# First norm's gain spread by TensorE into PSUM, the first v products issued singly, and a new order for the first stage

## The chip, the cores and the metric

The kernel runs on one core of one Trainium2 chip. A core has TensorE (PE; its weight loads are shown as PEld), VectorE (DVE), ScalarE (ACT), GpSimd (POOL) and SyncE (SP), which here only issues transfers; 16 DMA engines move data between HBM and SBUF. TensorE writes to PSUM, eight banks of 128 x 512 fp32 words. The metric is the device time of one execution in microseconds. Lower is better.

## The reference, cut to what matters

One layer of a decoder trunk over 1024 tokens of width 1024, all in float32:

```python
h = rms_norm(x, norm1_g)                       # x * rsqrt(mean(x*x) + eps) * g
q, k, v, glu_a, glu_b = split(h @ w_in)        # 512 columns each
attn = stick_breaking_attention(norm(q), norm(k), v)       # 8 heads x 64, causal
c = silu(layer_norm(causal_depthwise_conv(glu_a * sigmoid(glu_b))))   # width 31
x = x + concat([attn, c]) @ w_out
h = rms_norm(x, norm2_g)
gate, val = split(h @ w_up)                    # 2816 columns each
x = x + (silu(causal_dwconv3(gate)) * val) @ w_down
```

## The kernel before

Tokens lie in eight tiles of 128 (`t`), the model width in eight tiles of 128 (`k`). Every float32 product is made of three float32r matmuls (`mm3`, lines 387 to 390): each operand is split into a high part (`hi`, a cast on ACT) and a low part (`lo`, the source less the high part, on DVE or POOL), and hi x hi, hi x lo and lo x hi are added up in PSUM. So a product cannot run before the parts that it reads are made.

The first stage, up to about 420 us, holds the first norm, the five input projections, the convolution, the attention and the convolution's half of the output projection. After it come the second norm with the rest of the output projection, then the up projection (`u`, `u_S`) and the down projection (`dn`), each by a recursive block scheme.

At the start the gain of the first norm, one row of 4 KB in HBM, is read once for each of the 128 partitions (line 445), which is a transfer of 512 KB on ACT's queue into `g1`. PE meanwhile runs 16 idle matmuls on zeros (line 477). SP issues the loads of the eight tiles of x (`load_x`, line 485, 512 KB each) and of the weights (`weights`, line 538, 512 KB for each of the four v weights). A token tile then goes through `norm_in` (line 488): ACT squares it with a running sum (L494), into the tiles `attn` and `attn_first` in turn, which are scratch at that time; POOL makes the reciprocal root (`rstd`, L379 and L380); DVE scales the whole tile by the root and by `g1` (L498, 1024 elements in a partition); PE transposes it in two groups of four (L507); ACT copies each group out as the high part (L511), and DVE subtracts for the low part (L512). `weights` casts the high part on ACT (L542) and makes the low part on DVE or POOL (L547).

`project` (line 653) multiplies a token tile with the weights. For each of the eight `k` it adds one operation of three matmuls, which waits for the weight's low part (`ready`) and for the low part of that half of h. The v result goes out of PSUM in one copy of two pieces (L592).

The order of the work in the first two stages is written out. Each operation is given to a planner (`Plan`, line 146) with an engine or a choice of engines, a cost, what it waits for and the buffers it takes (`Token`). The planner's `run` goes through a table of operation numbers (`ORDERS`, line 61), which count in the order of `add`, picks an engine and a buffer by its costs, and emits. Within PE, DVE, ACT and POOL the emitted order is then fixed (`in_order`). The costs decide only engine and buffer; waits on the chip come from the data.

The banks named `z` (two) carry the convolution's two running sums (`conv_a`, L762) and later the attention's scores; `s` (three) carry transposes, `o` (three) the projections.

Of the kernel before, what the change touches and what calls it, by code (L numbers as in the profile page):

```python
# [8 lines left out]
F32 = mybir.dt.float32  # L9
# [24 lines left out]
CONV_AT = 52  # L34
V_AT = (12, 17.5, 45, 50.5, 78, 83.5, 89, 94.5)
# [235 lines left out]
def kernel(  # L271
# [192 lines left out]
    def in_order(start_at):  # L464
        last = {}
        for ins in nc.cur_bb.bb.instructions[start_at:]:
            if ins.engine in ORDERED:
# [3 lines left out]
                last[ins.engine] = ins  # L471

    start_at = len(nc.cur_bb.bb.instructions)
    idle = ps_.tile([P, 4, P], F32, tag="s2", name="idle")

    for i in range(16):
        nc.tensor.matmul(idle, ident_b, zero_b.unsqueeze(1).to_broadcast([P, 4, P]), start=True, stop=True)
# [1479 lines left out]
```

## Time and profile before

| | us |
|---|---|
| median of 3 runs | 1114.17 (1113.96 to 1115.74) |
| the profiled execution | 1114.16 |
| its span | 1112.4 |
| TensorE busy | 1092.3, 98% of the span |
| VectorE busy | 885.6, 80% |
| ScalarE busy | 608.7, 55% |
| GpSimd busy | 565.6, 51% |

The profile shows one execution. A line such as L498 is a line of the kernel before. Busy PE counts idle matmuls too, and it counts a matmul longer while PE's clock is granted at half rate. Matmuls are pipelined: their durations overlap, so the distance from start to start is what one costs. A stretch's row gives the length, then each engine's busy time and number of instructions, the granted PE clock, the share of time in which the DMA engines were busy, and GB/s. A piece of the chain of waits is a start, a length and the work that ended last.

### The profile page before, as it was taken

Reading aid. Unit: us, or ns where it says so; the run is one execution under the profiler, and the core shown is the slowest. Engines: PE = TensorE matmul, PEld = TensorE weight load, DVE = VectorE, ACT = ScalarE, POOL = GpSimd, SP = SyncE. Lnnn points to the kernel's source line nnn. Section 1 sums busy time; section 2 is a strip of 40 time slices with the busy share of each in tenths; the row PEclk is TensorE's granted clock in tenths of the full one; section 3 lists DMA queues with packets and bytes.
Section 4 is the critical chain, followed back from the end, with each engine's and each line's share of the span. In section 5 each row is a group of like instructions: output and inputs, shape, how many; then the busy total and the mean of one; then the engine's idle time right before and its main releaser. Section 6 shows DMA issues by size and latency. Waiting matters only on the chain.

```text
span 1112.4 us, 14919 instructions
## 1 busy us (share of the span) xinstructions
PE 1092.3 (98%) x5255; PEld 907.1 (82%) x5255; DVE 885.6 (80%) x1181; ACT 608.7 (55%) x1139; POOL 565.6 (51%) x509
## 2 busy tenths in 40 slices
PE   7999999999999999989999999999999999999998
PEld 5887888778888887768888888888888888888887
DVE  5587999679997996988886777677777578797795
ACT  6354467897766674654343434333333388776660
POOL 3064579677455452765333133223322199888770
PEclk9999999999999999999999999999999999999999
DMA  8111410353824216532322222223132482403404
GB/s 295 38 32 29 123 39 5 91 173 87 268 72 150 86 44 203 170 95 77 114 84 87 77 95 76 95 65 106 58 99 72 152 321 77 151 20 133 151 4 149
DMA packets 110233, 118.52 MB, mean 107 GB/s; under 512 B 21105, under 2 KB 89936, under 8 KB 110158
## 3 DMA queue, kind: packets, MB, share of 16 engines
q1 hardware_dynamic: 110014, 117.05, 32.1%
q8 instruction: 41, 0.67, 0.3%
q10 hardware_dynamic: 144, 0.52, 0.1%
q14 instruction: 34, 0.28, 0.1%
HBM read 82.95 MB, written 28.31 MB: 100 GB/s over the span
## 4 chain that ended last, share of the span: by engine, by line
PE 86%; POOL 5%; DVE 3%; ACT 2%; issue 2%; DMA 1%; SPq 0%; POOLq 0%; DVEq 0%; ACTq 0%
PE dn L1916 19%; PE u_S L388 7%; PE u_S L390 7%; PE u_S L389 7%; PE u L390 5%; PE u L389 5%; PE u L388 5%; PE po L1315 3%; POOL attn L789 3%; PE wT L1287 3%; PE z L1238 2%; PE z L1239 1%; PE op L388 1%; PE op L389 1%; PE op L390 1%
## 5 line engine op out<-in xcount | busy, mean ns | idle before, releaser
L1916 PE MATMUL dn<-wd,wd 128*128 128x512 f32 x768 | 181.4, 389 | 0.0
L1916 PEld LDWEIGHTS dn<-wd,wd 128*128 128x128 f32 x768 | 144.1, 188 | 29.9
L1919 DVE TENSOR_TENSOR c<-dn,c 128x512 f32<-128x512 f32 x120 | 81.7, 687 | 27.4 <-PE dn L1916 26.7
L389 PE MATMUL u_S<-bT,aS 128*128 128x512 f32 x264 | 102.7, 389 | 0.0
L390 PE MATMUL u_S<-bT,aS 128*128 128x512 f32 x264 | 102.7, 389 | 0.0
L388 PE MATMUL u_S<-bT,aS 128*128 128x512 f32 x264 | 102.4, 389 | 0.0
L384 ACT CAST aS<-rawu 128x512 fp32r<-128x512 f32 x63 | 38.9, 621 | 95.0 <-PE u_S L390 67.6
L1821 ACT CAST wd<-rawd 128x512 fp32r<-128x512 f32 x128 | 72.7, 618 | 31.8 <-DMA rawd<-act_d 8.4
L1260 DVE TENSOR_TENSOR_SCAN nb<-nb,one 128x896 f32<-128x896 f32 (+7 forms) x64 | 85.1, 1342 | 1.6 <-ACT nb L1246 1.3
L1662 POOL TENSOR_TENSOR s<-rawu 128x512 f32<-128x512 f32 x21 | 29.5, 1406 | 95.0 <-DMA rawu<-in_w_up_dram 93.8
L1820 ACT COPY whole<-rawd 128x512 f32<-128x512 f32 x110 | 63.4, 585 | 24.6 <-DVE wd L1822 11.9
L1668 POOL TENSOR_TENSOR rawu<-rawu 128x512 f32<-128x512 f32 x21 | 28.4, 1354 | 86.7 <-DVE a L385 86.7
L1822 DVE TENSOR_TENSOR wd<-whole,wd 128x512 fp32r<-128x512 f32 x90 | 60.1, 686 | 12.5 <-ACT wd L1821 6.2
L789 POOL TENSOR_TENSOR attn<-attn,attn_first 128x512 f32<-128x512 f32 x42 | 48.5, 1156 | 40.8 <-ACT attn L779 32.4
L390 PE MATMUL u<-b,a 128*128 128x512 f32 x168 | 65.5, 390 | 1.5 <-DVE a L385 1.5
L1265 POOL TENSOR_SCALAR nb<-nb 128x896 f32<-128x896 f32 (+7 forms) x52 | 37.6, 724 | 57.3 <-DVE nb L1260 44.7
L1765 DVE SCALAR_TENSOR_TENSOR y<-gv,cols_a,y 128x1023 f32<-128x1023 f32 (+1 forms) x44 | 59.2, 1345 | 8.5 <-ACT y L1763 8.4
L388 PE MATMUL u<-b,a 128*128 128x512 f32 x168 | 65.5, 390 | 0.0
L389 PE MATMUL u<-b,a 128*128 128x512 f32 x168 | 65.4, 389 | 0.0
L384 ACT CAST a<-rawu 128x512 fp32r<-128x512 f32 x63 | 39.0, 620 | 45.6 <-PE u_S L390 31.8
L390 PEld LDWEIGHTS u_S<-bT,aS 128*128 128x128 f32 x264 | 49.6, 188 | 10.3
L389 PEld LDWEIGHTS u_S<-bT,aS 128*128 128x128 f32 x264 | 49.5, 188 | 10.3
(339 smaller groups left out, 3239.0 us busy)
## 6 DMA issues: line engine op xcount, KB each, us to landing
rawu<-in_w_up_dram SPq DMA_DIRECT2D x44, 512.0 KB
act_d<-y SPq DMA_DIRECT2D x22, 512.0 KB
rawd<-act_d SPq DMA_DIRECT2D x22, 512.0 KB
rawd<-in_w_down_dram SPq DMA_DIRECT2D x22, 512.0 KB
raw_qk<-in_w_in_dram SPq DMA_DIRECT2D x16, 256.0 KB
rawo<-in_w_out_dram SPq DMA_DIRECT2D x8, 512.0 KB
m<-conv_d SPq DMA_DIRECT2D x16, 256.0 KB
xt<-in_x_dram SPq DMA_DIRECT2D x8, 512.0 KB
```

The lines of the kernel that those rows point to most:

```text
L384: nc.scalar.copy(hi, src)
L388: nc.tensor.matmul(ps, a_hi, b_hi, start=first, stop=False)
L389: nc.tensor.matmul(ps, a_hi, b_lo, start=False, stop=False)
L390: nc.tensor.matmul(ps, a_lo, b_hi, start=False, stop=last)
L789: last = add("POOL", 1092, lambda e=e: nc.gpsimd.tensor_tensor(d["c"], d["c"], e["t"], op=ALU.add), key(m, 16), [x, last])
L1260: nc.vector.tensor_tensor_scan(rev, rev, ones_of[0][:, :w], 0.0, op0=ALU.mult, op1=ALU.max)
L1765: nc.vector.scalar_tensor_tensor(y[:, j:], g[:, :S - j], par("fw", (KF - 1 - j) * NF + f), y[:, j:], op0=ALU.mult, op1=ALU.add)
L1820: nc.scalar.copy(whole, src)
L1821: nc.scalar.copy(t[:, 0], src)
L1822: lo_engine.tensor_tensor(t[:, 1], whole, f32(t[:, 0]), op=ALU.subtract)
L1916: nc.tensor.matmul(ps, a[:, tok], b, start=first and m == 0, stop=last and m == 2, skip_group_check=True)
L1919: nc.vector.tensor_tensor(sums[c][s], ps, sums[c][s], op=ALU.add)
```

## The change

- The gain is loaded as one row into partition 0 (`gain`), and a row of 128 ones (`gain_one`) is set by DVE. Two fp32 matmuls of one partition multiply the ones with each half of the row, so that each of the two `z` banks holds half of the gain on all partitions. PE runs five idle matmuls ahead of them and two behind, as the plan's first operation (`begin`), in place of the 16.
- `norm_in` scales a token tile in two halves of 512 elements, on DVE, with the gain read from PSUM; each half has its own transposes behind it.
- For token tiles 0 and 1 the v products are 24 single matmuls each, which wait only for the parts that they read (`high` or `ready` of the weight, `h_high` or `h_ready` of h). After the first, their order is free, and the copy out waits for all of them.
- The table of the first stage is new: 1915 numbers for 1874. Through the operations that are added, most numbers shift; the order changes in the whole stage. The table of the second stage stays.
- Some of the planner's costs change: the first transfer's start (4200 to 2900), a weight piece's issue, latency and transfer, and the costs of the two operations that take the attention result out of PSUM.

```diff
+SINGLE = (0, 1)
...
-    ROWS, PIECE, COLUMNS, MIXED, TWICE, FEW = (360, 1500, 1300), (430, 2000, 770), (390, 2050, 1650), (460, 2200, 870), (630, 1950, 450), (450, 1900, 50)
+    ROWS, PIECE, COLUMNS, MIXED, TWICE, FEW = (360, 1500, 1300), (430, 2200, 800), (390, 2050, 1650), (460, 2200, 870), (630, 1950, 450), (450, 1900, 50)
...
-    g1, sums_b = attn_row(0), attn_row(3)[:, S - P:]
-    nc.scalar.dma_start(g1, norm1_g.to_broadcast([P, D]))
+    sums_b = attn_row(3)[:, S - P:]
+    gain, gain_one = attn_row(3)[0:1, :], attn_row(2)[0:1, :P]
+    nc.scalar.dma_start(gain, norm1_g)
+    nc.vector.memset(gain_one, 1.0)
...
-                 in_turn=("nb", "wt", "th", "tl", "thd", "tld", "kst", "vst", "q", "qd"), dma=4200.0)
+                 in_turn=("nb", "wt", "th", "tl", "thd", "tld", "kst", "vst", "q", "qd"), dma=2900.0)
...
-    idle = ps_.tile([P, 4, P], F32, tag="s2", name="idle")
-    for i in range(16):
-        nc.tensor.matmul(idle, ident_b, zero_b.unsqueeze(1).to_broadcast([P, 4, P]), start=True, stop=True)
+    g1 = []
+    def begin():
+        idle = ps_.tile([P, 4, P], F32, tag="s2", name="idle")
+        def wait(n):
+            for _ in range(n):
+                nc.tensor.matmul(idle, ident_b, zero_b.unsqueeze(1).to_broadcast([P, 4, P]), start=True, stop=True)
+        wait(5)
+        for i, z in enumerate(gain_banks):
+            g1.append(bank(z, [P, HS], f"gain{i}"))
+            nc.tensor.matmul(g1[i], gain_one, gain[:, i * HS:(i + 1) * HS], start=True, stop=True)
+        wait(2)
...
+    gain_banks = [plan.token("z") for _ in range(2)]
+    gain_ready = add("PE", 6300, begin, -100.0, [], gain_banks)
...
-        c = add("DVE2", 1290, lambda: nc.vector.scalar_tensor_tensor(xt, xt, d["rs"], g1, op0=ALU.mult, op1=ALU.mult), T(at_), [b])
...
         for i in range(2):
+            cols = slice(i * HS, (i + 1) * HS)
+            c = add("DVE", 690, lambda i=i, cols=cols: nc.vector.scalar_tensor_tensor(xt[:, cols], xt[:, cols], d["rs"], g1[i], op0=ALU.mult, op1=ALU.mult),
+                    T(at_), [b, gain_ready])
+            gain_banks[i].users += [c]
...
+        singles = []
+        for k, which in ((k, which) for k in range(ND) for which in ("hh", "hl", "lh") if name == "v" and t in SINGLE):
+            def product(k=k, which=which):
...
+                nc.tensor.matmul(d["ps"], (h_hi if which[0] == "h" else h_lo)[t // 4][:, k, tok],
+                                 ws[k // 2]["hi" if which[1] == "h" else "lo"].rearrange("p k b c -> p k (b c)")[:, k % 2, :],
+                                 start=d["n"] == 1, stop=d["n"] == 3 * ND)
+            needs = [ws[k // 2]["high" if which[1] == "h" else "ready"], (h_high if which[0] == "h" else h_ready)[t][k // 4]]
+            singles.append(add("PE", 227, product, T(at_ + 0.7 * k), needs + singles[:1], [] if singles else [o]))
...
-                a = add("ACT", 580, copied, i + 0.3, [last, prev_last] + conv_normed + (on_diagonal[0] if blk else []))
-                b = add("DVE", 690, summed, i + 0.3, [a])
+                a = add("ACT", 690, copied, i + 0.3, [last, prev_last] + conv_normed + (on_diagonal[0] if blk else []))
+                b = add("DVE", 790, summed, i + 0.3, [a])
```

More of the change, by code (lines that the diff above doesn't have):

```diff
@@ L473 @@
     start_at = len(nc.cur_bb.bb.instructions)
-    idle = ps_.tile([P, 4, P], F32, tag="s2", name="idle")
-    for i in range(16):
-        nc.tensor.matmul(idle, ident_b, zero_b.unsqueeze(1).to_broadcast([P, 4, P]), start=True, stop=True)
+    g1 = []
[9 more added lines that the diff above has]
+        wait(2)
     done, big, nbs, ones_of, qkv = {}, {}, [None] * 4, [], {}
-    h_ready = {}
+    gain_banks = [plan.token("z") for _ in range(2)]
+    gain_ready = add("PE", 6300, begin, -100.0, [], gain_banks)
+    h_ready, h_high = {}, {}
     def load_x(t, key):
@@ L497, in norm_in @@
         b = add("POOL", 850, lambda: rstd(d["rs"], d["sq"], 1.0 / D), T(at_), [a])
-        c = add("DVE2", 1290, lambda: nc.vector.scalar_tensor_tensor(xt, xt, d["rs"], g1, op0=ALU.mult, op1=ALU.mult), T(at_), [b])
-        r.users += [c]
-        h_ready[t] = []
+        h_ready[t], h_high[t] = [], []
         for i in range(2):
+            cols = slice(i * HS, (i + 1) * HS)
+            c = add("DVE", 690, lambda i=i, cols=cols: nc.vector.scalar_tensor_tensor(xt[:, cols], xt[:, cols], d["rs"], g1[i], op0=ALU.mult, op1=ALU.mult),
+                    T(at_), [b, gain_ready])
+            gain_banks[i].users += [c]
+            r.users += [c]
             s = plan.token("s")
@@ L509, in norm_in @@
             where = (slice(None), slice(4 * i, 4 * i + 4), slice((t % 4) * P, (t % 4 + 1) * P))
-            a = add("PE", 440, turn, T(at_ + 1), [c], [s])
-            b = add("ACT", 600, lambda i=i, where=where: nc.scalar.copy(h_hi[t // 4][where], d["pt", i]), T(at_ + 1), [a])
+            m = add("PE", 440, turn, T(at_ + 1), [c], [s])
+            f = add("ACT", 600, lambda i=i, where=where: nc.scalar.copy(h_hi[t // 4][where], d["pt", i]), T(at_ + 1), [m])
             e = add("DVE", 690, lambda i=i, where=where: nc.vector.tensor_tensor(
-                h_lo[t // 4][where], d["pt", i], f32(h_hi[t // 4][where]), op=ALU.subtract), T(at_ + 1), [b])
-            s.users += [b, e]
+                h_lo[t // 4][where], d["pt", i], f32(h_hi[t // 4][where]), op=ALU.subtract), T(at_ + 1), [f])
+            s.users += [f, e]
             h_ready[t].append(e)
-        norm_done.append(a)
+            h_high[t].append(f)
+        norm_done.append(m)
     norm_done = []
@@ L549, in weights @@
         room.users += [x, a, b]
-        d["ready"] = b
+        d["high"], d["ready"] = a, b
         return d
@@ L653, in project @@
     def project(name, parts, ws, t, at_, room):
-        o, d, m = plan.token("o"), {}, None
+        o, d, m = plan.token("o"), {"n": 0}, None
         tok = slice((t % 4) * P, (t % 4 + 1) * P)
-        for k in range(ND):
+        singles = []
+        for k, which in ((k, which) for k in range(ND) for which in ("hh", "hl", "lh") if name == "v" and t in SINGLE):
+            def product(k=k, which=which):
+                if d["n"] == 0:
+                    d["ps"] = bank(o, [P, 512], f"{name}{t}")
+                    room()
+                d["n"] += 1
+                nc.tensor.matmul(d["ps"], (h_hi if which[0] == "h" else h_lo)[t // 4][:, k, tok],
[3 more added lines that the diff above has]
+            singles.append(add("PE", 227, product, T(at_ + 0.7 * k), needs + singles[:1], [] if singles else [o]))
+            for r in ws[k // 2]["rooms"]:
+                r.users += singles[-1:]
+        for k in range(ND if not singles else 0):
             def products(k=k):
@@ L675, in project @@
             return (summed if t in SUMMED_FIRST else normalized)(f"{name}{t}", d, o, m, to, at_ + 6)
-        a = add({"ACT": 700, "DVE": 800}, lambda eng: copy_out(eng, to(), d["ps"]), T(at_ + 6), [m])
+        a = add({"ACT": 700, "DVE": 800}, lambda eng: copy_out(eng, to(), d["ps"]), T(at_ + 6), singles or [m])
         o.users += [a]
```

146 rows, old and new, of the table ORDERS are left out of this document.

## The prediction

> **What bounds the kernel now.** I read the page's busy table first, then the table of stretches, then the chain of waits in the first 22 us, then the timeline there. The page and the stretches (columns: stretch, its length, busy time of PE, PEld, DVE, ACT, POOL with counts, granted clock, DMA share, GB/s):
>
> ```profile
> PE 1092.3 (98%) x5255; PEld 907.1 (82%) x5255; DVE 885.6 (80%) x1181; ACT 608.7 (55%) x1139; POOL 565.6 (51%) x509
> ```
>
> ```profile
> 0.00:10.00 10.00, 5.11 (x16) 1.87 (x16) 1.77 (x6) 4.29 (x7) 2.51 (x10) 1.00 0.79 272
> ...
> 30.00:100.00 70.00, 69.80 (x323) 57.28 (x322) 48.72 (x69) 25.77 (x45) 21.05 (x19) 1.00 0.11 31
> 100.00:120.00 20.00, 19.31 (x86) 15.66 (x85) 19.54 (x24) 13.02 (x20) 17.76 (x15) 1.00 0.36 99
> ...
> 200.00:300.00 100.00, 97.18 (x578) 82.31 (x578) 84.69 (x116) 83.29 (x205) 64.64 (x78) 1.00 0.50 156
> 300.00:400.00 100.00, 99.95 (x662) 88.80 (x662) 89.17 (x109) 69.15 (x143) 50.65 (x58) 1.00 0.32 96
> 400.00:500.00 100.00, 94.06 (x473) 77.22 (x472) 84.51 (x113) 56.72 (x108) 53.60 (x56) 0.98 0.45 142
> ```
>
> ```profile
> 10.14:21.52 11.38, 9.75 (x45) 7.34 (x45) 10.71 (x10) 8.55 (x14) 6.59 (x6) 0.85 1.05 384
> ...
> 22.00:70.00 48.00, 48.00 (x231) 39.57 (x230) 30.89 (x44) 22.51 (x38) 11.80 (x17) 1.00 0.17 48
> ```
>
> TensorE is the bound, with some 20 us of gaps in the span of 1112.4 us. Half of these lie ahead of 21.52 us, and those gaps are understated: the 5.11 us of the first row are idle matmuls, and the second table's clock of 0.85 over 11.38 us means 3.4 us at half rate. From 21.52 us PE runs without a gap to 70 us. So the first question is when PE becomes unbroken, and how much useful work it has done by then. The chain of waits of the first 23 us (start, length, what):
>
> ```profile
> 1.54 6.35 issue
> ...
> 8.21 0.57 POOL rs L380
> 8.78 0.03 issue
> 8.80 1.29 DVE x_k L498
> 10.10 0.04 issue
> 10.14 0.67 PE hT L507 x4
> ...
> 17.45 1.81 DVE x_q L498
> ...
> 20.79 0.69 DVE h_lo L512
> ```
>
> The first token tile's square (below) starts at 6.70, when x0 lands; its norm feeds the first transposes at 10.14. The last stall ends at 21.52, behind a scaling of x that held DVE from 17.45 on. In the timeline (start, length, engine, line, what, [idle before and releaser]):
>
> ```profile
> 6.70 1.06 ACT L494 ACTIVATE attn<-x_k 128x1024 f32<-128x1024 f32 x1 [4.05 <-DMA x_k<-in_x_dram]
> 7.94 1.06 ACT L494 ACTIVATE attn_first<-x_k 128x1024 f32<-128x1024 f32 x1
> 9.50 1.05 ACT L542 CAST hi_v<-raw_v 128x1024 fp32r<-128x1024 f32 x1 [0.41 <-DMA raw_v<-in_w_in_dram]
> 10.58 1.23 DVE L547 TENSOR_TENSOR lo_v<-raw_v,hi_v 128x1024 fp32r<-128x1024 f32 x1 [0.49 <-ACT hi_v L542]
> 10.83 0.59 ACT L511 CAST h_hi<-hT 128x512 fp32r<-128x512 f32 x1 [0.29 <-PE hT L507]
> 11.47 0.76 PE L388 MATMUL v<-hi_v,h_hi 128*128 128x512 f32 x1 [0.24 <-ACT h_hi L511]
> 11.72 0.68 DVE L512 TENSOR_TENSOR h_lo<-hT,h_hi 128x512 fp32r<-128x512 f32 x1
> 17.38 2.40 POOL L547 TENSOR_TENSOR lo_v<-raw_v,hi_v 128x1024 fp32r<-128x1024 f32 x1
> 17.45 3.42 DVE L498 SCALAR_TENSOR_TENSOR x_q<-x_q,rs,attn 128x1024 f32<-128x1024 f32 x1
> ```
>
> ```profile
> 22.71 0.60 PE L507 MATMUL hT<-ident_r,x_q 128*128 128x128 f32 x4
> 23.07 0.48 PE L388 MATMUL v<-hi_v,h_hi 128*128 128x512 f32 x1
> ...
> 24.08 0.39 PE L389 MATMUL v<-lo_v,h_hi 128*128 128x512 f32 x1
> 24.31 0.39 PE L390 MATMUL v<-hi_v,h_lo 128*128 128x512 f32 x1
> ```
>
> By start to start, a product costs 0.23 us and a group of four transposes 0.36. The 45 PE instructions between 10.14 and 21.52 are 24 transposes and 21 products: 6 x 0.36 + 21 x 0.23 = 7.0 us of work. So at 21.52 PE has lost 21.52 - 7.0 = **14.5 us**. The forecast is this loss after the change.
>
> **The change, part by part.** *The gain's load.* The spread row (queue q10) goes through the same 16 engines as x0. Bytes by queue in 2 to 6 us, then the total of 6 to 14 us:
>
> ```profile
> q1 hardware_dynamic: 175, 0.66, 48.6%
> q10 hardware_dynamic: 138, 0.51, 34.5%
> ```
>
> ```profile
> DMA packets 2028, 3.07 MB, mean 383 GB/s; under 512 B 146, under 2 KB 1657, under 8 KB 2028
> ```
>
> Without its 0.51 MB all loads behind come 0.51 / 383 = 1.33 us earlier at the most; at the least 0, if x0 is held by start-up and not by rate. DMA was full from 4 us on, so I take 1.25.
>
> *The gain's matmuls.* Sixteen idle matmuls become five, two gain products, two more idle ones: by the diff fewer idle matmuls, whatever the summary says.
>
> ```profile
> 1.68 5.11 PE L477 MATMUL idle<-zero_b,ident_b 128*128 128x512 bf16 x16 [1.68 <-DVE ident_b L341]
> ...
> 3.36 0.15 PEld L477 LDWEIGHTS <-ident_b 128*128 128x128 bf16 x1 [0.28 <-issue]
> 3.79 0.15 PEld L477 LDWEIGHTS <-ident_b 128*128 128x128 bf16 x1 [0.28 <-issue]
> ```
>
> At first they come 0.43 apart, so five end at 3.8. No row has a one-partition f32 product. Bounds: 0.23 each (a warm product) and 1.7 (four times the slow idle one). The plan's cost for the whole block is 6.3 us, which less seven at 0.43 leaves 1.65 each; I take that, near the upper end. Then the block ends at about 7.7, ahead of the first transposes below (8.35), so it costs nothing; this cover is 0.6 us. DVE's scaling, which is wanted at 7.55, needs only the gain products (about 7.1). Were the row to land as late as x0 (5.45), the scaling would wait until 8.8 and everything behind it 1.2 us. The second square writes where the row of ones lay, so ACT waits for those matmuls too, with the cast of the first v weights queued behind; it is due at 6.70, so up to 0.4 us may show. The memset falls into DVE's idle time ahead of 8.80.
>
> *Scaling in halves.* The nearest row is the second norm's, with its gain in PSUM (duration min/median/max):
>
> ```profile
> L1569 DVE SCALAR_TENSOR_TENSOR h<-x,rs,g x16: 731/740/749, 430.5 to 479.7; 128x512 f32<-128x512 f32 x16
> ```
>
> A half takes 0.74, so the first transposes come 1.28 - 0.74 = 0.54 earlier. A tile costs DVE 1.48 instead of 1.28: 0.8 us over the first four tiles, on the way to PE, and 0.8 over the rest, under unbroken PE. In return, the scaling that took 3.42 beside POOL's subtraction in SBUF now reads its gain from PSUM. The two banks are held until the eighth tile is scaled (39.0 us now), and the convolution needs them at 59.8:
>
> ```profile
> L498 DVE SCALAR_TENSOR_TENSOR x_qk<-x_qk,rs,attn x4: 1275/1276/1287, 28.5 to 39.0; 128x1024 f32<-128x1024 f32 x4
> ```
>
> ```profile
> L762 DVE SCALAR_TENSOR_TENSOR conv_a<-cpad,cols_b,conv_a x60: 744/756/757, 59.8 to 180.4; 128x512 f32<-128x512 f32 x60
> ```
>
> *Single products and the order of the start.* For token tiles 0 and 1 all 48 v products stand alone, hi-by-hi ones needing no low part. The new table loads x0, x1, then all four v weights, then x3 and x2 (now x3 and x2 stand ahead of the third weight). The steps, each by the durations above: x0 lands 5.45; square to DVE takes 8.80 - 6.70 = 2.10, so the first half is scaled 7.55 to 8.29 and the transposes start at 8.35. The v weight is cast 8.25 to 9.3, then the first high part of h to 9.9, then PE's first product (11.47 now). In the table's order ACT goes on with the second v weight (11.0), a half of tile 1 (11.6), the second half of tile 0 (12.2), the third and fourth weight (13.25, 14.3). POOL makes low parts at 2.40 each from 9.4, DVE at 1.23 after its four scalings and three halves of h_lo (13.0). PE does four groups of transposes and two products by 11.55 (1.9 us of work); from there I followed its listed products against these times, and each is ready when its turn comes. x3 and x2 come two loads later but 1.25 us earlier for the lighter queue, so about 1.4 us later in all; the 46 products left, 10.6 us, cover that.
>
> Loss: 11.55 - 1.9 = 9.65, plus 0.95 (0.8 for DVE's longer scaling, the rest for one low part that comes late) = **10.6 us**. Gain 14.5 - 10.6 = 3.9. The ends: 4.9 if nothing is late, 1.8 (1.25 + 0.54) if PE then stalls as often as now.
>
> *The clock.* The second table's 0.85 puts 3.4 us of the start at half rate, after an idle PE from 6.8 to 10.14. My steps have PE idle for about 0.6 us at 8 and half busy to 11.55, so I take a full clock. Were it half from 11 to 14.4, the work there would lose 1.7 us. The Trainium skill, "TensorE: Matmul & The Clock Gate", section "Part 1: The HAM clock gate (the "warmup" mystery)", speaks of a free-running window of about 3.4 us after whose idleness the clock halves, and its section "Part 4: PE-mode transpose" says that transposes do not count as busy in the same way. The 3.4 us agree with the trace; by that rule a window over 8 to 11.5, with little but transposes in it, could halve the clock again, and the sum would be the second rival's.
>
> *The rest of the table* reorders all of the first stage, to 420 us. Of 673 PE operations common to both and behind the first v products, 77 keep their place, and the mean shift is 6 places. The work is the same. Gaps there are few: 0.2 us in 30 to 100, 0.7, then 2.8 in 200 to 300. I put it at nothing, as PE is unbroken there, with -1.5 to +6 as its ends. The planner's other constants emit no instruction.
>
> The sum is against the profiled execution: 1114.16 us, span 1112.4, median of the runs 1114.17. **1114.16 - 3.9 = 1110.2 us.** Behind 30 us everything is paced by PE's results (DVE is 70% busy in 30 to 100), so I let the gain through; tail and up/down projections keep their order.
>
> **Rivals.**
>
> *The loss is only moved.* DVE's convolution is nearly full (19.54 of 20 us in 100 to 120, 84.69 in 200 to 300). If it sets when attention starts, PE just waits there. Against it: DVE idles in 30 to 100, so its chain starts earlier with PE. All lost: 1114; half: 1112.5. I put it at 1113.2.
>
> *The clock drops again, or only the lighter load counts.* 1110.2 + 1.7 = 1111.9; with 1.8 us alone 1112.4. It speaks for this that ACT, not PE, feeds the products until 14 us. I put it at 1112.0.
>
> *Slower: the new table starves PE in attention.* Between 200 and 300 us PE waits 2.8 us now, with DVE at 85% and ACT at 83%; a reordered split or copy is a PE wait at once. It decides from 3.9 us of new waits there. Three times today's waits, +5.7 us, gives 1110.2 + 5.7 = 1115.9; with the +6 above and a start that gains 1.8 it is 1118.4.
>
> **How the numbers follow.** Forecast 0.60 (its own range 1108.5 to 1111.9), clock or load 0.15, moved 0.13, slower 0.12. About 0.2% (2.2 us) can be told from no change: under 1111.9 counts as faster, over 1116.4 as slower. Faster: nearly all of the forecast and half of the second, 0.67. Slower: most of the last beyond its price, 0.08. Same: 0.25. The range goes from 1107.8 (4.9 at the start, 1.5 from the table) to 1114.0, which takes in the first two rivals.
>
> **What would show it.** First transposes at about 8.35, not 10.14; first v product at 9.9; PE unbroken from about 12; clock 1.00 in 10 to 15; gain products done before 7.5; scaling of 0.74 each, none near 3.4. Gaps in 30 to 420 of about 5 us as now. I am wrong if the first transposes come before 9 and the time still falls by less than 2 us: then look for the new gaps between 70 and 300.

## The result, and the profile after

The changed kernel takes **1108.35 us** (median of 4 runs, 1106.93 to 1109.83) beside 1114.95 us (4 runs) for the kernel before on the same chip: ratio 0.9943, 95% interval 0.9930 to 0.9957. It is 6.6 us faster; 3.9 were forecast. The profiled execution took 1108.51 us, its span is 1105.7 us (1112.4 before).

The page's busy table of the kernel after:

```profile
PE 1091.2 (99%) x5250; PEld 908.6 (82%) x5250; DVE 871.2 (79%) x1177; ACT 605.0 (55%) x1125; POOL 581.9 (53%) x517
```

The table of stretches of the kernel after (stretch, length, busy time of PE, PEld, DVE, ACT, POOL with counts, granted clock, DMA share, GB/s), and two rows of the same view of the kernel before with the same bounds:

```profile
10.00:20.00 10.00, 9.69 (x42) 7.89 (x41) 8.79 (x11) 8.04 (x13) 7.67 (x8) 1.00 0.91 351
20.00:30.00 10.00, 10.00 (x57) 8.36 (x56) 7.33 (x12) 7.64 (x13) 3.49 (x8) 1.00 0.43 120
30.00:100.00 70.00, 70.00 (x320) 57.51 (x319) 49.07 (x71) 28.32 (x49) 27.42 (x25) 1.00 0.13 38
...
200.00:300.00 100.00, 99.37 (x603) 84.99 (x603) 86.89 (x119) 80.97 (x191) 65.42 (x76) 1.00 0.52 156
300.00:400.00 100.00, 100.00 (x673) 90.48 (x672) 89.46 (x107) 72.76 (x150) 54.85 (x60) 1.00 0.31 96
400.00:500.00 100.00, 92.11 (x446) 75.12 (x445) 82.59 (x111) 54.02 (x101) 55.83 (x54) 0.98 0.40 132
```

```profile
10.00:20.00 10.00, 9.62 (x45) 7.34 (x45) 9.28 (x9) 8.59 (x14) 6.72 (x7) 0.83 1.05 391
20.00:30.00 10.00, 8.60 (x42) 7.09 (x42) 7.14 (x9) 7.33 (x14) 2.59 (x9) 1.00 0.66 189
```

PE has no gap from 20 to 100 us, the 2.8 us of gaps between 200 and 300 have shrunk to 0.6, and one stretch became worse: 400 to 500, with 7.9 us of gaps in place of 5.9.

Gaps are not the whole loss: a product counts as busy for 0.39 us, though the next one can start 0.23 us after it, so a wait of up to 0.16 us leaves no gap. So I extend the prediction's measure over the whole first stage: the start of a PE instruction less the useful work that stands ahead of it, each useful PE instruction counted by its columns at the distance from start to start at full clock (0.23 us for 512 columns, 0.36 for four transposes), idle and gain products at nothing. Worked out from all PE starts of each trace, in us; the first column is the label of a run told of below:

| kernel | at 30 us of work | at 100 | at 230 | at 380 | at 450 |
|---|---|---|---|---|---|
| before | 15.8 | 17.0 | 23.1 | 35.1 | 46.4 |
| after | 12.3 | 12.6 | 17.1 | 26.1 | 39.8 |
| a_new_start_old_rest | 12.5 | 17.5 | 23.3 | 35.5 | 48.1 |
| a2_new_to_100us | 11.9 | 12.2 | 18.9 | 31.0 | 42.1 |
| b_old_start_new_rest | 14.8 | 17.0 | 21.5 | 30.4 | 41.7 |
| d_banks | 11.8 | 12.1 | 16.6 | 25.6 | 36.5 |
| c_gain_spread_by_dma | 18.5 | 18.8 | 23.2 | 32.3 | 45.9 |
| g1_dma_gain_copied_to_psum | 11.5 | 11.8 | 16.3 | 25.3 | 36.5 |
| g2_matmul_gain_copied_to_sbuf | 18.0 | 18.3 | 22.8 | 31.8 | 41.7 |
| i_before_with_gain_in_psum | 15.1 | 16.4 | 21.5 | 33.6 | 45.0 |
| e_v_in_triples | 12.2 | 12.5 | 17.0 | 26.1 | 40.2 |
| f_ones_elsewhere | 11.1 | 11.4 | 15.9 | 25.0 | 38.6 |
| h_banks_and_ones | 11.7 | 12.0 | 16.5 | 25.5 | 36.6 |

Only differences between rows are read. The level hangs on the price of a product: with 0.227 in place of 0.230 us for 512 columns every row of the column at 380 comes out about 5.5 us higher, but before less after stays at 8.9 or 9.0. Each row is one trace, and two things differ between traces of the same start. One is when PE comes to full rate. In a, the kernel after, a2 and d, which begin alike, transposes follow each other at 0.21 us and products at 0.43 until 13.4, 13.1, 12.3 and 12.0 us, and at 0.11 and 0.23 from there; their losses at 30 us of work are 12.5, 12.3, 11.9 and 11.8, so a full clock that comes 1.4 us later costs 0.7. The fourth group of transposes in the kernel after and in d, in the timeline:

```profile
12.42 0.94 PE L527 MATMUL hT<-ident_r,x_k 128*128 128x128 f32 x4
```

```profile
12.22 0.60 PE L529 MATMUL hT<-ident_r,x_k 128*128 128x128 f32 x4
```

The other is told at b, whose start is that of before, with 14.8 in place of 15.8.

The first two rows give three parts. The start gains 3.5 us (15.8 - 12.3). Between 30 and 380 us of work the new order gains 5.5 more (19.3 lost there before, 13.8 after); it is split further below. And behind 380, at the handover from the first stage to the second, 2.4 are given back (11.3 lost before, 13.7 after). Sum 6.6. Forecast were the first part at 3.9 and nothing for the others.

The start of the kernel after, in the timeline (start, length, engine, line, what, [idle before and releaser]):

```profile
3.92 3.78 PE L491 MATMUL gain<-attn,attn_first 1*128 1x512 f32 x4
4.66 1.06 ACT L511 ACTIVATE attn<-x_k 128x1024 f32<-128x1024 f32 x1 [1.88 <-DMA x_k<-in_x_dram]
...
6.75 0.75 DVE L518 SCALAR_TENSOR_TENSOR x_k<-x_k,rs,gain 128x512 f32<-128x512 f32 x1 [5.00 <-POOL rs L383]
...
7.63 1.03 PE L486 MATMUL idle<-zero_b,ident_b 128*128 128x512 bf16 x2
7.74 1.06 ACT L511 ACTIVATE attn_first<-x_k 128x1024 f32<-128x1024 f32 x1 [1.93 <-PE gain L491]
7.74 0.75 DVE L518 SCALAR_TENSOR_TENSOR x_k<-x_k,rs,gain 128x512 f32<-128x512 f32 x1 [0.24 <-PE gain L491]
8.46 1.91 PE L527 MATMUL hT<-ident_r,x_k 128*128 128x128 f32 x8
...
9.83 1.41 DVE L518 SCALAR_TENSOR_TENSOR x_k<-x_k,rs,gain 128x512 f32<-128x512 f32 x2 [1.35 <-ACT hi_v L563]
9.90 4.74 POOL L568 TENSOR_TENSOR lo_v<-raw_v,hi_v 128x1024 fp32r<-128x1024 f32 x2
...
10.68 1.09 PE L527 MATMUL hT<-ident_r,x_k 128*128 128x128 f32 x4 [0.31 <-issue]
...
11.42 1.20 PE L685 MATMUL v<-hi_v,h_hi 128*128 128x512 f32 x2
```

x0 lands 2.0 us earlier (6.70 before). Each gain product is two instructions, and the four take 3.78 us, so ACT's second square waits 1.93 us for them. Yet DVE scales the second tile in 1.41 us right beside POOL's subtraction, and the first transposes start 1.7 us earlier than before (10.14). They could have come earlier still: their half of x is scaled by 7.50 us, but PE is at the gain products until 7.70 and then at the two idle matmuls, and starts them at 8.46.

At the handover, the chain that ended last in the kernel after (start, length, what):

```profile
410.49 1.00 DVE loo L1499
411.62 1.22 DVE loo L1499
412.87 0.71 DVE attn L1382
413.62 0.50 PE opa L391
```

PE's first product of the output projection (`opa`) waits 2.4 us for DVE, which makes two low parts first and only then takes the last attention result out of its PSUM bank (L1382). This wait is not in the kernel before, whose largest wait of `opa` is the third line:

```profile
PE u L393 <- DVE a L388: 2.7, 1, 2.7
PE opa L391 <- DVE attn L1382: 2.4, 1, 2.4
```

```profile
PE opa L388 <- DVE x L1551: 1.2, 2, 0.6
```

The first two lines are the kernel after's waits of PE, the third is the kernel before's (engine, line, releaser: us in total, times, longest). By the program's allocation, which the profile does not show, the changed kernel claims the gain's two banks right behind that of the idle matmuls and ahead of the five others, and so its banks stand in another order; the last attention result falls on the bank that `opa` takes first. Before, the two were different banks.

### The profile page after: what moved, and what is told of

Read it like the earlier page. It is cut to its first block, busy times and chain, and to the rows that moved or that the text cites. A ratio compares the mean times of both kernels' runs of the same rounds, so it can differ in the third digit from the quotient of the medians.

```text
span 1105.7 us, 14913 instructions
## 1 busy us (share of the span) xinstructions
PE 1091.2 (99%) x5250; PEld 908.6 (82%) x5250; DVE 871.2 (79%) x1177; ACT 605.0 (55%) x1125; POOL 581.9 (53%) x517
## 4 chain that ended last, share of the span: by engine, by line
PE 92%; POOL 3%; DVE 2%; ACT 1%; issue 1%; DMA 0%; POOLq 0%; DVEq 0%; ACTq 0%; SPq 0%
PE dn L1952 19%; PE u_S L391 7%; PE u_S L393 7%; PE u_S L392 7%; PE u L393 5%; PE u L391 5%; PE u L392 5%; PE po L1351 3%; PE wT L1323 3%; PE qk L392 2%; PE qk L391 2%; PE qk L393 2%; PE z L1274 2%; PE z L1275 2%; PE op L391 1%; POOL attn L825 1%
## 5 line engine op out<-in xcount | busy, mean ns | idle before, releaser
L1955 DVE TENSOR_TENSOR c<-dn,c 128x512 f32<-128x512 f32 x120 | 81.3, 685 | 25.6 <-PE dn L1952 25.3
L1296 DVE TENSOR_TENSOR_SCAN nb<-nb,one 128x640 f32<-128x640 f32 (+7 forms) x64 | 85.0, 1341 | 2.1 <-ACT nb L1282 1.9
L1856 ACT COPY whole<-rawd 128x512 f32<-128x512 f32 x110 | 63.4, 585 | 24.1 <-DVE wd L1858 11.3
L1858 DVE TENSOR_TENSOR wd<-whole,wd 128x512 fp32r<-128x512 f32 x90 | 59.9, 683 | 14.8 <-ACT whole L1856 7.4
L1301 POOL TENSOR_SCALAR nb<-nb 128x1024 f32<-128x1024 f32 (+7 forms) x54 | 38.7, 720 | 56.1 <-DVE nb L1296 51.8
L1700 POOL TENSOR_TENSOR rawu<-s,rawu 128x512 f32<-128x512 f32 x21 | 31.8, 1513 | 51.6 <-DVE a L388 50.8
L391 PEld LDWEIGHTS u_S<-bT,aS 128*128 128x128 f32 x264 | 50.0, 189 | 10.4
L825 POOL TENSOR_TENSOR attn<-attn 128x512 f32<-128x512 f32 x25 | 33.3, 1332 | 47.2 <-ACT attn L815 29.5
```

Of the source, the lines that this page charges most:

```text
L391: nc.tensor.matmul(ps, a_hi, b_hi, start=first, stop=False)
L825: last = add("POOL", 1092, lambda e=e: nc.gpsimd.tensor_tensor(d["c"], d["c"], e["t"], op=ALU.add), key(m, 16), [x, last])
L1296: nc.vector.tensor_tensor_scan(rev, rev, ones_of[0][:, :w], 0.0, op0=ALU.mult, op1=ALU.max)
L1856: nc.scalar.copy(whole, src)
L1858: lo_engine.tensor_tensor(t[:, 1], whole, f32(t[:, 0]), op=ALU.subtract)
L1955: nc.vector.tensor_tensor(sums[c][s], ps, sums[c][s], op=ALU.add)
```

## The experiments

All times are medians, with the ratio to the kernel before on the same chip (1113.7, 1113.8, 1114.4 and 1113.6 us in the four sets).

### Start and rest apart

**a_new_start_old_rest.** The changed kernel, whose order is its own for the first 197 numbers; what is left follows in the order of the kernel before. The five other PSUM banks are claimed first, so that the bank order is that of before.

```diff
+        for tag in ("s0", "s1", "o0", "o1", "o2"):
+            ps_.tile([P, 512], F32, tag=tag, name=f"claim_{tag}")
-the table: numbers 198 to 1915 in the new order
+the table: numbers 198 to 1915 in the order of the kernel before
```

> The kernel after up to the point where the first two token tiles' v products and all norms are in the list (197 operations); behind it the order of the kernel before. The PSUM banks are laid out as before (the projections' and transposes' banks claimed first). Theory 1, start and rest are separate gains: by equal work done PE is 3.4 us ahead of before at 30 us and nothing is added later, so about 1110.8 us, with the gaps of before between 100 and 300 us (glu_b behind lo_glu_b, qk behind lo_qk, kT behind the queries' low part). Rival 2, the later gaps shrink because the start is earlier, whatever the order: 1106 to 1108.5, gaps gone. Rival 3, the start is paced by what comes later: no lead at 100 us, 1114.

Measured: 1114.64 us, ratio 1.0007 (0.9998 to 1.0016). The start is there (12.5 at 30 us of work), and is lost by 100 us (17.5). PE's waits of this kernel show where:

```profile
PE glu_a L392 <- DVE lo_glu_a L569: 1.6, 1, 1.6
PE glu_b L390 <- ACT cpad L774: 1.4, 1, 1.4
```

Neither wait is in the kernel before or after: the seam made them, by joining two orders in the middle of the first weights. The time says nothing on the rest.

**b_old_start_new_rest.** The kernel before, whose table goes on in the order of the changed kernel behind its operation 143.

```diff
-the table: the order of the kernel before
+the table: behind operation 143, the order of the changed kernel
```

> The kernel before, with its own start (143 operations), and behind it the order of the new table; its banks are its own, so the last attention result does not lie in the bank that the next stage takes first. Theory 1: first transposes at 10.1 us as before, PE's loss by equal work as before up to 30 us, then a lead that grows to about 5 us at the end of the first stage, of which some 0.8 is lost in the second norm: about 1109.4 us. Rival 2, the order behind the start is worth nothing by itself: 1114.

Measured: 1109.60 us, ratio 0.9966 (0.9954 to 0.9979), 4.1 us under the kernel before. The loss from 100 to 380 us of work is that of after (13.4 and 13.5), not that of before (18.0). So the new order of the rest is worth something by itself. Gaps show where more than half of that comes from (100 to 400 us; the kernel before, then the kernel after):

```profile
100.00:400.00 300.00, 296.43 (x1678) 252.69 (x1677) 267.98 (x351) 216.72 (x486) 191.62 (x199) 1.00 0.34 102
```

```profile
100.00:400.00 300.00, 299.05 (x1719) 257.72 (x1718) 262.11 (x344) 216.08 (x481) 203.24 (x203) 1.00 0.35 106
```

The gaps fall from 3.57 to 0.95 us, and to 0.91 in b: 2.6 of the 4.5 us. From start to start, between 100 and 380 us of work, 14 PE instructions are over 0.17 us late before (5.4 us in all) and 9 in the kernel after (2.6). Some hundred smaller delays, of 0.06 to 0.17 us, cost about 9 us in both: most of what PE loses while busy, the new order leaves as it is.

Up to 44 us b and before run the same instructions in the same order on every engine, and yet b loses 1.0 less at 30 us of work. In the trace of before POOL's subtraction began at 17.38 and DVE's scaling at 17.45, and the scaling took 3.42 us. In b DVE came first, and it is POOL's subtraction, 2.40 before, that takes 3.42:

```profile
17.15 1.28 DVE L498 SCALAR_TENSOR_TENSOR x_q<-x_q,rs,attn 128x1024 f32<-128x1024 f32 x1
17.28 3.42 POOL L547 TENSOR_TENSOR lo_v<-raw_v,hi_v 128x1024 fp32r<-128x1024 f32 x1 [0.17 <-ACT hi_v L542]
```

PE's stall of 1.40 us behind that scaling, the last of the start, is not there in b. At 100 us of work the lead is gone (17.0 both).

**a2_new_to_100us.** As a, with the cut behind 404 numbers, about 100 us into the stage.

```diff
-the table: numbers 198 to 1915 in the order of the kernel before
+the table: numbers 405 to 1915 in the order of the kernel before
```

> As the first of these runs (new start, old order behind it, banks as before), but the cut lies where PE has done about 95 us of work (404 operations) and not 45. There the mixed order had stalled PE twice just behind its seam (glu_b behind a copy on ACT queued behind a weight's cast, glu_a behind a low part queued behind the convolution). Theory 1, start and rest are separate and those stalls were of the seam: PE is 4.5 to 5 us ahead of before at 100 us, keeps that lead through the old order, and the time is about 4 us under before's (1109.5 where before is 1113.7). Rival 2, the old order gives the lead back wherever the seam lies: within 1 us of before.

Measured: 1110.61 us, ratio 0.9969 (0.9959 to 0.998). At this cut the start's lead survives (12.2 at 100), and then the old order loses as it did before: 18.8 us from 100 to 380 (18.0 before, 13.5 after). Its waits of PE have the old rows again:

```profile
PE kT L1197 <- DVE rest L1238: 0.8, 1, 0.8
PE z L1275 <- ACT nb L1283: 0.7, 2, 0.4
PE qk L391 <- DVE lo_qk L569: 0.6, 1, 0.6
```

The first of them is gone in the kernel after, the others are down to 0.3. So the new list up to 100 us is worth 3.2 us here (1113.8 - 1110.6), and the kernel after, which is faster, has the rest from the order behind it.

### The wait at the handover

**d_banks.** The changed kernel, with the five other banks claimed first, so that the bank order is that of before.

```diff
+        for tag in ("s0", "s1", "o0", "o1", "o2"):
+            ps_.tile([P, 512], F32, tag=tag, name=f"claim_{tag}")
```

> The kernel after with one thing changed: the banks of the transposes and projections are claimed ahead of the two gain banks, so that the layout is that of before and the last attention result no longer lies in the bank that the output projection takes first. Theory: the wait of 2.4 us between the last attention product and the first product of the next stage falls to under 0.5, and the time by about 2 us against the kernel after, to 1106.3. Rival: that product waits for the attention's data (its sum on DVE), not for the bank: wait and time unchanged, 1108.3.

Measured: **1104.19 us**, ratio 0.9917 (0.9903 to 0.993), against 0.9943 (0.9930 to 0.9957) for the kernel after: 2.9 us by the ratios, with intervals that just touch. The wait of 2.4 us is gone from its waits of PE, and the first `opa` product starts at 410.6 instead of 413.6 (duration min/median/max, first and last start):

```profile
L391 PE MATMUL opa<-hio,m x38: 388/389/477, 410.6 to 440.0; 128*128 128x512 f32 x38
```

```profile
L391 PE MATMUL opa<-hio,m x35: 388/390/500, 413.6 to 439.9; 128*128 128x512 f32 x35
```

The first fence is d, the second the kernel after. With a2, which differs from d only in the order behind 100 us, the order of the rest is worth 1110.6 - 1104.2 = 6.4 us (5.8 by the ratios, 0.9969 and 0.9917). That is more than b's 4.1, in which the seam costs something: b loses 2.2 us between 30 and 100 us of work, the kernel after 0.3.

### The gain: its load or its place

**c_gain_spread_by_dma.** The changed kernel, with the gain's 512 KB load as before; the halves are scaled with the gain in SBUF, and there are 16 idle matmuls and no gain products.

```diff
-    nc.scalar.dma_start(gain, norm1_g)
-    nc.vector.memset(gain_one, 1.0)
+    g1_row = attn_row(0)
+    nc.scalar.dma_start(g1_row, norm1_g.to_broadcast([P, D]))
...
-            g1.append(bank(z, [P, HS], f"gain{i}"))
-            nc.tensor.matmul(g1[i], gain_one, gain[:, i * HS:(i + 1) * HS], start=True, stop=True)
+            bank(z, [P, HS], f"gain{i}")
+            g1.append(g1_row[:, i * HS:(i + 1) * HS])
```

> The kernel after, but the gain is loaded as before, 512 KB spread over the partitions, into SBUF; PE runs 16 idle matmuls and no gain products, DVE scales in halves from SBUF. Order and banks as after. Theory 1, the lighter load is worth about what x0 comes earlier, less what the gain products cost ACT: x0 lands at 6.5 instead of 4.7, first transposes at 9.6 instead of 8.5, the second square no longer waits for PE (1.9 us now); PE's loss at 30 us some 1.2 us higher, time up by about 1.2 against the kernel after. Rival 2, ACT's wait on the gain products ate the whole gain of the lighter load: within 0.4 us of after. Rival 3, the load is the whole start: up by 3 us.

Measured: 1113.74 us, ratio 0.9993 (0.9984 to 1.0002), all of the gain lost. The cost is not where I looked for it. x0 lands at 6.74, but the loss is 18.5 at 30 us of work, more than before. In the timeline:

```profile
10.64 5.11 POOL L567 TENSOR_TENSOR lo_v<-raw_v,hi_v 128x1024 fp32r<-128x1024 f32 x2
10.70 5.60 DVE L517 SCALAR_TENSOR_TENSOR x_k<-x_k,rs,attn 128x512 f32<-128x512 f32 x2 [0.45 <-POOL rs L383]
...
13.61 0.42 PEld L526 LDWEIGHTS hT<-ident_r,x_k 128*128 128x128 f32 x4 [2.88 <-issue]
...
14.02 1.05 PE L684 MATMUL v<-hi_v,h_hi 128*128 128x512 f32 x2
```

Two halves of a scaling that took 1.41 us in the kernel after take 5.60 here, beside the same two subtractions on POOL, and the first v product starts at 14.02 instead of 11.42. Then PE's clock falls to half for 6.8 us:

```profile
14.19:21.01 6.82, 4.93 (x15) 3.54 (x14) 6.82 (x8) 6.63 (x11) 4.00 (x4) 0.50 1.01 393
```

This run changes the load and the gain's place at once; the next two part them, both with the banks claimed as in d (1104.19 us).

**g1_dma_gain_copied_to_psum.** The heavy load and 16 idle matmuls, then DVE copies the gain into the two banks.

```diff
-            nc.tensor.matmul(g1[i], gain_one, gain[:, i * HS:(i + 1) * HS], start=True, stop=True)
+            nc.vector.tensor_copy(g1[i], g1_row[:, i * HS:(i + 1) * HS])
```

> The kernel with the banks claimed (1104.2 us), but with the gain loaded to all 128 partitions (512 KB) as before, and then copied by VectorE into the same two PSUM banks, so that the scaling reads its gain from PSUM; 16 idle matmuls as before. Theory one, that the scaling with both operands in SBUF is what GpSimd's subtraction of the v weights holds up: the heavy load costs only its 2 us of x's landing and the copies at most 0.7 more, the second tile's two scalings take about 1.4 us together beside GpSimd and not 5.6, PE's loss at 30 us is about 14.5 (12.3 + 2.1, no more than 15.5), and the time 1106.4. Theory two, that the heavy load itself is what costs 5.5 us (its place in the queue delays x and the v weights): the loss stays at 18.5 and the time is 1110.

Measured: 1104.71 us, ratio 0.9911 (0.9898 to 0.9925). From d's 0.9917 it can't be told: theory one, and more than it asked for, as the heavy load costs nothing that shows (loss 11.5 at 30 us of work, 14.5 expected). Its x0 lands at 6.40 (4.36 in d) and its first transposes start at 9.30 (8.46), but the second tile's scaling starts at 9.82 (9.84), since here ACT's second square does not wait for gain products, and PE, at full rate from the first transposes on, starts the first v product at 11.04 (11.43). Its rows for the first pair of tiles:

```profile
L528 PE MATMUL hT<-ident_r,x_k x16: 272/273/328, 9.3 to 12.3; 128*128 128x128 f32 x16
L519 DVE SCALAR_TENSOR_TENSOR x_k<-x_k,rs,gain x4: 739/740/746, 8.5 to 10.5; 128x512 f32<-128x512 f32 x4
```

**g2_matmul_gain_copied_to_sbuf.** The light load and the gain products, then DVE copies the gain from PSUM to SBUF, and the scaling reads it there.

```diff
+            gb = bank(z, [P, HS], f"gain{i}")
+            nc.tensor.matmul(gb, gain_one, gain[:, i * HS:(i + 1) * HS], start=True, stop=True)
+            g1.append(attn_row(0)[:, i * HS:(i + 1) * HS])
+            nc.vector.tensor_copy(g1[i], gb)
```

> The kernel with the banks claimed (1104.2 us), with the gain as one row and two matmuls into PSUM as in the changed kernel, but VectorE then copies both halves to SBUF (0.7 us each, the second one on the path of the first transposes) and the scaling reads its gain from there. Theory one (two operands in SBUF beside GpSimd's subtraction): the second tile's scalings take 4 to 5.6 us together again, PE's loss at 30 us rises from 12.3 to about 16.5, and the time is 1108.5. Theory two (only the load matters): the loss rises by the copy alone, to 13.0, and the time is 1104.9.

Measured: 1110.38 us, ratio 0.9966 (0.9954 to 0.9979), 6.2 us over d; theory one again, with more loss than it asked for (18.0, not 16.5). The same view:

```profile
L531 PE MATMUL hT<-ident_r,x_k x16: 421/421/476, 9.1 to 17.2; 128*128 128x128 f32 x16
L522 DVE SCALAR_TENSOR_TENSOR x_k<-x_k,rs,attn x4: 741/1789/2851, 8.3 to 13.0; 128x512 f32<-128x512 f32 x4
```

A half takes 0.74 us alone and 2.85 beside POOL: longer by 2.11, a little less than one POOL subtraction (2.40), as if DVE's instruction were held until POOL's ends. The Trainium skill, "SBUF — State Buffer", section "Who interferes with whom", says so: a VectorE instruction with two SBUF inputs contends with a GpSimd instruction that reads SBUF, and whichever started first holds the shared port for its whole length. The trace agrees, by these 2.85 and 0.74 us, and by before and b above, where once DVE and once POOL was held.

The held scalings are not all of the 6.2 us. By PE's starts against d, the two copies put the first transposes 0.7 later (9.14), PE's two waits behind the held halves take 3.5 more than in d, and 2.0 goes because PE runs at half rate until 20.4 us, in d until 12.0. A v product in g2 and one in d:

```profile
18.66 0.63 PE L689 MATMUL v<-hi_v,h_lo 128*128 128x512 f32 x1
```

```profile
13.35 0.40 PE L687 MATMUL v<-hi_v,h_lo 128*128 128x512 f32 x1
```

No run parts the late clock from the waits.

**i_before_with_gain_in_psum.** The kernel before, with the place changed: its order, its heavy load, and a copy into the two banks; the five other banks are claimed first. The scaling comes in two halves with it.

```diff
+    g1 = [ps_.tile([P, HS], F32, tag=f"z{i}", name=f"gain{i}") for i in range(2)]
+    for i in range(2):
+        nc.vector.tensor_copy(g1[i], g1_row[:, i * HS:(i + 1) * HS])
...
+            for i in range(2):
+                cols = slice(i * HS, (i + 1) * HS)
+                nc.vector.scalar_tensor_tensor(xt[:, cols], xt[:, cols], d["rs"], g1[i], op0=ALU.mult, op1=ALU.mult)
```

> The kernel before, with its order, its heavy load of the gain and its 16 idle matmuls, and one edit: VectorE copies the gain from SBUF into the two PSUM banks, and the scaling reads it there, in two instructions of 512 columns one behind the other (1.48 us in place of 1.28 us). So the placement of the gain alone, without the new order. Theory one, that the lock between VectorE's second SBUF operand and GpSimd's subtraction matters only where the order puts such a pair on the path of the first products: the row of 3.42 us for the fourth scaling (2.1 us over its sister) goes, PE's loss at 30 us falls from 15.8 to no less than 14.5, and the time is 1113.0 to 1114.2. Theory two, that the placement by itself is the gain of the start: the loss at 30 us falls by 3 us or more and the time is 1111 or less.

Measured: 1112.49 us, ratio 0.9991 (0.9982 to 1.0), 0.5 us under theory one's range and far from theory two's. The loss at 30 us of work is 15.1 against 15.8, and the long scaling is gone (mean 743 ns for each half of x_q; one tile took 3.42 us before):

```profile
L507 DVE SCALAR_TENSOR_TENSOR x_q<-x_q,rs,gain 128x512 f32<-128x512 f32 x4 | 2.8, 743 | 0.0
```

So neither half of the start is worth much alone. The place without the new order gives about 1 us, which its interval hardly tells from nothing (i). The new order, which sets POOL to two low parts right where DVE scales the second tile, loses 6.2 us without the place (g2 against d), or 5.5 if the copies' 0.7 us are left out.

### Single products, and the row of ones

**e_v_in_triples.** The changed kernel, in which the v products of tiles 0 and 1 stand in the table by `k`, three at a time, and each keeps its place behind the one before. The wait for both low parts is the planner's alone: on the chip a product waits for the data that it reads, as the first one below shows.

```diff
-            needs = [ws[k // 2]["high" if which[1] == "h" else "ready"], (h_high if which[0] == "h" else h_ready)[t][k // 4]]
-            singles.append(add("PE", 227, product, T(at_ + 0.7 * k), needs + singles[:1], [] if singles else [o]))
+            needs = [ws[k // 2]["ready"], h_ready[t][k // 4]]
+            singles.append(add("PE", 227, product, T(at_ + 0.7 * k), needs + singles[-1:], [] if singles else [o]))
...
-the table: the v products of tiles 0 and 1 in the order of the kernel after
+the table: these products by k, in the same places
```

> The kernel after, but the v products of token tiles 0 and 1 go in k's order, three at a time, and all wait for both low parts, in the places of the list that their tile's single products had. Theory 1, singles only fill the first microseconds: first product at 12.3 (behind the first low part, which POOL ends at 12.3) instead of 11.4, one more wait of about 1 us behind the second weight's low part; time up by 1 to 1.5 us. Rival 2, singles are most of the start's gain: first 10 us of work 3 us later, time up by 3.

Measured: 1109.01 us, ratio 0.9951 (0.9939 to 0.9964), against 0.9943 (0.9930 to 0.9957) for the kernel after; the loss at 30 us of work is 12.2 against 12.3. The first product does not wait for the low part, which POOL begins at 9.90 and has at 12.3; the second one does, 0.3 us:

```profile
11.42 0.57 PE L684 MATMUL v<-hi_v,h_hi 128*128 128x512 f32 x1
...
12.32 0.50 PE L684 MATMUL v<-lo_v,h_hi 128*128 128x512 f32 x1 [0.34 <-POOL lo_v L567]
```

So e tests the free order of the products and not their finer waits, and it shows no worth of that order. Nor does it show that there is none: PE came to full rate at 11.6 us here and at 13.1 in the kernel after, which, by the runs of the same start above, may be worth some 0.7 us at 30 us of work.

**f_ones_elsewhere.** The row of ones lies where the second square does not write.

```diff
-    gain, gain_one = attn_row(3)[0:1, :], attn_row(2)[0:1, :P]
+    gain, gain_one = attn_row(3)[0:1, :], attn_row(0)[0:1, :P]
```

> The kernel after, with the row of ones in a place that no square writes (the row where the gain lay before), so ACT's second square no longer waits for the gain products. Theory 1, that wait (1.9 us in the profile of after) is the start's new bound: second square at 5.9 instead of 7.7, first cast of v at 7.5 to 8 instead of 8.8, first product before 10.2 instead of 11.4, time down by about 1 us. Rival 2, the first cast waits for its own load and PE's gain block ends at 8.4 in any case: the wait moves to the load or the transposes, time within 0.3 us of after.

Measured: 1106.62 us, ratio 0.9937 (0.9925 to 0.9949). The second square starts at 5.86, not at 7.74, and the first v product at 10.73, not at 11.42; the loss at 30 us of work is 11.1 against 12.3. But PE came to full rate at 10.6 us here, at 13.1 in the kernel after, which by itself may be worth that much. The intervals overlap with the kernel after's, so the gain in time is not settled.

**h_banks_and_ones.** Both mends, d's and f's.

```diff
-    gain, gain_one = attn_row(3)[0:1, :], attn_row(2)[0:1, :P]
+    gain, gain_one = attn_row(3)[0:1, :], attn_row(0)[0:1, :P]
...
+        for tag in ("s0", "s1", "o0", "o1", "o2"):
+            ps_.tile([P, 512], F32, tag=tag, name=f"claim_{tag}")
```

> Both mends in one: the five banks are claimed as in the kernel before, and the row of ones lies where the second token tile's square does not write. The mend of the banks alone took 1104.2 us; the mend of the ones alone lowered PE's loss at 30 us from 12.3 to 11.1 us. If the order's later waits leave that lead alone, this kernel takes 1104.2 - 1.2 = 1103.0 us. Rival: a wait later in the first stage that does not depend on PE's position takes the lead back, and the time stays at 1104.2.

Measured: **1102.88 us**, ratio 0.9894 (0.9879 to 0.9909), the lowest median of the study. Against f (0.9937, 0.9925 to 0.9949) the intervals lie apart, so the order of the banks shows its worth a second time, 4.8 us by the ratios. Against d they overlap. As a time h is what theory one asked for, but the loss at 30 us of work is 11.7 against d's 11.8. The trace shows why: the first v product starts at 10.88, 0.55 earlier than in d, but PE comes to full rate at 12.4 instead of 12.0, and the first product that both run at full rate starts at 12.51 here and at 12.58 in d. So the 1.3 us between the medians of h and d can't be put down to the row of ones.

## Why the prediction was right, and where it was wrong

**The measure held, and the total was in part luck.** Counting what PE has lost by the time that it becomes unbroken gave the start: forecast 14.5 to 10.6, gain 3.9; measured 15.8 to 12.3 at 30 us of work, gain 3.5, and 3.2 by a2's time. That the whole came to 6.6 and stayed near the forecast is luck: 5.5 us that I had put at nothing came on top, and 2.4 that I had not seen went off again.

**The steps under it held less well.** *First transposes* 8.35, measured 8.46, by luck: the first half of x was scaled by 7.50, and PE's own gain block held them. In all seven traces that read the gain from PSUM by the light load they start at 8.46, whether x0 lands at 4.36 (d) or 4.66 (the kernel after). I had the block end at 7.7 and cost nothing; by my own numbers (7.1 and two idle matmuls at 0.43) it was 8.0. *Scaling in halves* at 0.74, none near 3.4: measured 0.75, none. *The second square* was to be held by the gain products by up to 0.4; it was held 1.93, since the products came at 3.92 to 7.70 and x0 already at 4.66, not 5.45. Their price, 1.65 us each, was 1.89. *The first v product* was put at 9.9 and came at 11.42: PE's order has three groups of transposes ahead of it, the third for the second tile, whose scaling, behind the held square, started at 9.83. *PE unbroken* from 11.55: its last gap ends already at 10.68, but it runs at full rate only from 13.1. *The clock* was to be full from 10 to 15 us, and was not, although the table of stretches shows 1.00: the 16 transposes of the first two tiles, of which g1's median is 273 ns, take 421 in the kernel after (duration min/median/max):

```profile
L527 PE MATMUL hT<-ident_r,x_k x16: 304/421/448, 8.5 to 13.1; 128*128 128x128 f32 x16
```

From 10.68 to 13.1 PE does 1.2 us of work, eight transposes and two products, in 2.4, so the half rate costs at most 1.2 us there. And of the 20 us of gaps before, not half but a third lies ahead of 21.52 by the rows shown (6.7 us); it is over half only with the idle matmuls' 5.1 us.

**The load's term was mis-sized.** 1.25 us for the lighter queue: x0 came 2.0 earlier, but g1, with the heavy load, takes d's time. The way in which the light load is spread takes the 2.0 us back: PE's gain block leaves 0.84 of them at the first transposes (8.46 in d, 9.30 in g1), ACT's wait for the gain products leaves none at the second tile's scaling, and at half rate the first v product comes later than with the heavy load (11.43 and 11.04). f takes ACT's wait away alone; the block and the clock were not parted.

**The gain's place had no term.** I quoted the row of 3.42 us beside POOL's 2.40 and wrote that the scaling now reads from PSUM, but gave it no price of its own. In the new order it carries 5.5 to 6.2 us (g2 against d), of which 2.0 went by way of PE's clock. The forecast of the sum stood only because I took the durations of an unhindered scaling, 0.74.

**The rest of the table at nothing was the failed step.** Its reason was few gaps and PE unbroken, but the rows that I quoted hold 3.7 us of gaps (0.2, 0.7 and 2.8), and I set the end at -1.5. At the price used here PE lost 18.0 us in all from 100 to 380 us of work, most of it while it counted as busy; the new order lost 13.5. Of these 4.5, 2.6 were gaps that the rows showed, and the rest left no gap. In time the order of the rest is worth 4.1 us (b) to 6.4 (a2 against d), beyond the end that I had set. Why this list waits less, one wait at a time, was not tried.

**The give-back was not foreseen.** The rival "the loss is only moved" was right that something would be waiting for PE, but it named DVE's convolution and attention; there PE's listed waits fell from 3.4 us (100 to 400) to 0.8. The new wait stood at the handover, 2.4 us, by a PSUM bank that the change of the allocation's order had brought there; d shows it by taking it away. The slower rival, a starved PE in 200 to 300, was not seen: its gaps shrank from 2.8 to 0.6. Of the clock rival the half rate was true; its price of 1.7 us was at most 1.2 behind the last gap, and lies inside the measured gain of the start. Single products, which stood in my steps as ready products without a price, gave nothing that shows (e).

## What to carry to other kernels

A short row next to a long one of the same instruction (0.74 and 2.85, or 1.28 and 3.42) is a price list: ask what ran beside the long one, which of the two began first, and where the new order will put such a pair. Cost a new order by what PE has lost at equal work, from the start times, and not by the gaps in a busy share alone. Before two single traces are compared at the start, look when each came to full rate. And when a change claims a buffer first, look at which buffers all later claims then fall on, above all where one stage hands over to the next.

## What the runs showed of the hardware that was not expected

- A VectorE scaling with both tensors in SBUF takes 2.85 us instead of 0.74 beside one GpSimd subtraction in SBUF; with the gain in PSUM it takes 0.74 to 0.75 beside the same subtraction (g2, g1 and the kernel after). In two traces of the same list the one that began second was held: DVE's scaling in the kernel before (3.42 for 1.28, 0.07 us behind POOL), POOL's subtraction in b (3.42 for 2.40, 0.13 us behind DVE).
- One fp32 product of one partition and 512 columns comes out as two instructions and takes 1.89 us at the start of the kernel (3.78 for two). In the eight traces with those products PE's clock was not yet full when the transposes began (421 ns in the kernel after and in g2); it came up between 10.6 us (f) and 20.5 (g2), at another time in each trace of the same start. After 16 unbroken idle matmuls it was full (273 ns, g1). Whether the products or the fewer idle matmuls are the cause was not tried.
- The column of the granted clock shows 1.00 in 8 to 13 us of the kernel after, where the transposes' durations say that it was lower.
